# RWKV's main streams on TensorE in the order of the source, with the projections between them left free

## The chip, the cores and the metric

The kernel runs on one core of one Trainium2 chip. The metric is the device time of one execution in microseconds. The kernel before took 1292.87 us, the median of three runs (1289.9 to 1293.16 us). TensorE is called PE below, VectorE DVE, ScalarE ACT, GpSimd POOL and SyncE SP.

## The reference

One step of a one-layer hybrid encoder for 1024 prompt frames and 64 sample frames (with 512 cached ones). All branch columns come from one projection of the normalised input; three branches are gated and projected back:

```
u = rms_norm(h); z = u @ w_in                      # (1088, 1024) @ (1024, 5836)
A: RWKV-7 mixing, 8 heads of 64: a delta-rule state S (64 x 64 per head), frame by frame
     S = S * w_t + (S @ -kk_t) (kk_t * a_t)^T + v_t k_t^T ;  y_t = S @ r_t
B: forgetting attention (FoX), 8 heads, softmax(q k / 8 + c_t - c_s), s <= t
C: indexer scores, the top 256 keys of each frame, softmax attention over them with a T5 bias
h = h + concat(y_A * silu(g_A), y_B * silu(g_B), y_C * silu(g_C)) @ w_out ; y = rms_norm(h)
```

Outputs are y for prompt and sample, the new states and the new cache rows.

## The kernel before

**Stages.** After the input norm comes the indexer, then the RWKV stage with the top-k search beside it, then FoX, then the sparse attention and the output projection. The change concerns the RWKV stage.

**Projections.** `proj` (L154) multiplies 128 columns of w_in with 384 or 320 frames. For each of eight slices of 128 input features it issues three matmuls, a triple: bf16 weights with the low part of u, then the high and the low part of the weights with the high part of u. After a triple the generator yields. Projections wait in the deque `fill`; `pump(n)` adds n to a credit and issues one triple for each whole credit. In the RWKV stage's braids the credit grows by 0.7 per step, and by more in the last braids.

**RWKV in chunks.** The recurrence is computed in chunks of 64 frames, four chunks of one pair of heads to a unit: 16 units for the prompt and one for the sample. Each unit goes through five streams, written as generators: the preparation (`prep`: element-wise work on decay, rates and keys in `elem`, then the chunk's products in `chunk_rows`), `value_rows` (`rows`), the inversion of a triangular 64 x 64 matrix by doubling (`invert`, five levels), the sequential `chain` over the four chunks, and the `tail` with the group norm. In `invert`, PE products (L1500, L1507, transposes L1514) alternate with DVE updates of U, T and Y (L1538, L1543, L1547). In `chain` each chunk has three steps: L1588 and DVE's za (L1589); L1593 and DVE's copies of UV (L1598); and then

```
matmul(ch[.., c*64 ..], BA.., UV..)                        # L1601, both halves
scalar_tensor_tensor(self.state, ch[.., c*64 ..], ..)      # L1606, DVE
matmul(py = ch[.., 256 + c*64 ..], BA.., UV..)             # L1610, same PSUM bank as ch
matmul(py, QR.., S)                                        # L1612
```

Most fp32 matmuls stand twice in the profile, so that L1601 and L1610 have four entries for each chunk. The products of `elem`, `chunk_rows` and `value_rows` use one PSUM bank in turn (`ps_ga`), some of them `ps_tp`; the inversion has two (`ps_gb`).

**The braid.** `program` runs 19 braids. In braid u stand the tail of unit u-2, the chain of u-1, the inversion and the value rows of u, and the preparation of u+1. `braid` deals their steps by fractions: step k of a stream with n steps has the place (k + 0.5)/n, with n = 3 for the tail, 12 for the chain, 14 for the inversion, 10 for the preparation (it uses eight), and 2 for the value rows (place times 0.4). After each step come `note` and `pump`, and steps of the top-k search on DVE and ACT. The first preparation runs alone in a `weave`.

**What sets the order on an engine.** The program is not issued in the order of the source. The framework keeps a priority for each instruction (its place in the source) and orders each engine's queue by its own estimate of when operands and buffers are ready: the ready instruction of the highest priority first. Order edges constrain it: an edge says that one instruction stands behind another on its engine, without a wait. `tied` gives the instructions of a projection step a priority 1000 places later and ties the first PE instruction to the last one of the stream whose step came before (`behind`, which `note` keeps). So a projection does not stand ahead of that point, and may stand later. Between the main streams there is one set of edges: `in_order(at)` after L1442 keeps eight products of `chunk_rows` in their order.

Of the kernel before, what the change touches and what calls it, by code (L numbers as in the profile page):

```python
# [85 lines left out]
class K:  # L86
# [96 lines left out]
    def note(self, label):  # L183

        ins = self.nc.cur_bb.bb.instructions
        for i in ins[self.seen:] if label in TIES or not TIES else ():
            self.behind.setdefault(i.engine, {})[label if TIE else 0] = i.name
        self.seen = len(ins)

    def in_order(self, n):  # L190

        last = None
        for i in self.nc.cur_bb.bb.instructions[n:]:
            if i.engine == PE:
                if last is not None:
                    self.tc.add_manual_dep(i, last, mybir.DependencyInfo(
                        mybir.DependencyClass.NoSync, mybir.DependencyReason.DATA), reason="order of issue")
                last = i.name

    def pump(self, n):  # L200

        self.credit = min(self.credit + n, 8)
        while self.credit >= 1 and self.fill:
            self.mark(self.fill[0][0])
            if self.tied(self.fill[0][1], (PE,)):
                self.credit -= 1
            else:
                self.filled.add(self.fill.popleft()[0])
# [1201 lines left out]
    def chunk_rows(self, one, x):  # L1410

        nc = self.nc
        v, g, sc = nc.vector, nc.gpsimd, nc.scalar
        G = self.gring("ga", 1)
        QR, BK, ND = x["QR"], x["BK"], x["ND"]
        dg = self.dg

        BA = one.tile([P, 2, 4, 128], F32, tag="BA", name="BA", bufs=3)  # L1420
        BN = one.tile([P, 2, 4, 64], F32, tag="BN", name="BN", bufs=NBN)
        lo, hi = hv = (slice(0, 64), slice(64, 128))
        p1 = G()
        for c in range(4):
            self.turn(p1[:, c * P:c * P + P], BK[:, c, 0:2].rearrange("p a t -> p (a t)"))
        q1 = p1.rearrange("p (c h d) -> p c h d", h=2, d=64)
        sc.copy(BA[:, 0, :, 0:64], q1[:, :, 0])
        sc.copy(BA[hi, 1, :, 64:128], q1[lo, :, 1])
        sc.copy(BA[lo, 1, :, 64:128], q1[hi, :, 1])
        yield  # L1430
        am = self.con[:, C_AM:C_AM + P].rearrange("p (o x t) -> p o x t", o=1, x=2)
        ps = self.tp()
        nc.tensor.matmul(ps[:, :256], self.ones[:, C_BD - C_M:C_N - C_M], x["rk"], start=True, stop=True)
        x["vb"] = vb = one.tile([P, 4, 64], F32, tag="vb", name="vb", bufs=4)
        v.scalar_tensor_tensor(vb, ps[:, :256].rearrange("p (c t) -> p c t", t=64), 0.5, QR[:, :, 2], op0=OP.mult, op1=OP.mult)
        yield

        pm = G(), self.tp()
        at = len(nc.cur_bb.bb.instructions)
        for c in range(4):  # L1440
            for h in range(2):
                nc.tensor.matmul(pm[h][:, c * P:c * P + P], BK[hv[h], c, h:h + 2].rearrange("p a t -> p (a t)"),  # L1442
                                 QR[hv[h], c, 0:2].rearrange("p a t -> p (a t)"), start=True, stop=True)
        self.in_order(at)
        for h in range(2):
            q = pm[h].rearrange("p (c x t) -> p c x t", x=2, t=64)
            for i, dst in ((1, BN[:, h]), (0, BA[:, h, :, 64 - 64 * h:128 - 64 * h])):
                v.tensor_tensor(dst, q[:, :, i], am[:, :, i].broadcast_to([P, 4, 64]), op=OP.mult)
            g.tensor_scalar(dg(ND[:, 0], h), BN[hv[h], h], 1.0, 0.0, op0=OP.mult, op1=OP.add)
            g.tensor_tensor(dg(ND[:, 1], h), BN[hv[h], h], dg(ND[:, 0], h), op=OP.subtract)  # L1450
            if h == 0:
                yield
        x.update(BA=BA, BN=BN)
        yield
# [330 lines left out]
def program(ctx, tc, I, O):  # L1785
    s = K(ctx, tc, I, O)
    s.pproj = s.pool("pproj", bufs=2, space=PSUM)
    s.ptp = s.pool("ptp", bufs=1, space=PSUM)
    s.banks = itertools.cycle((s.proj_bank, s.proj_bank, s.tp))
    s.keep = s.pool("keep")  # L1790
    s.dram = s.pool("dram", space=DRAM)
    s.d_g = s.dram.tile([1024, NT], F32, tag="d_g", name="d_g")
    s.d_y = s.dram.tile([2, 4, P, NT], F32, tag="d_y", name="d_y")
    s.cp = s.pool("const")
    c1 = ExitStack()
    uw = s.pool("uw", ctx=c1)
    s.uH = uw.tile([P, KD, NT], F32R, name="uH")
    s.uL = uw.tile([P, KD, NT], BF16, name="uL")
    s.wraw = s.pool("wraw", bufs=NW, ctx=c1)
    s.wsp = s.pool("wsp", bufs=2, ctx=c1)  # L1800
    s.zp = s.pool("zp", bufs=2, ctx=c1)
    ci = ExitStack()
    s.ip = s.pool("idx", ctx=ci)
    s.ip2 = s.pool("idx2", bufs=2, ctx=ci)
    cx = ExitStack()
    s.load_x(cx)
    s.mark('norm')
    s.norm_in()
    s.mark('setup')
    s.setup()  # L1810
    cx.close()
    with ExitStack() as c2:
        s.lr = s.pool("lr", ctx=c2, right=True)
        s.zs = s.pool("zs", bufs=1, ctx=c2, right=True)
        s.scp = s.pool("scp", ctx=c2, right=True)
        s.tkp = s.pool("tkp", ctx=c2, right=True)
        s.junk = s.pool("junk", ctx=c2, right=True)
        s.free = True
        s.weave(("idx", s.indexer()), R_IDX[0], R_IDX[1])
        ci.close()  # L1820
        s.rwkv_pools(c2)
        s.need("a0")
        s.free = False
        for nm, w, j in (("a2", s.park_a, 2), ("a3", s.park_a, 3), ("b0", s.park_b, 0),
                         ("b1", s.park_b, 1), ("b2", s.park_b, 2), ("b3", s.park_b, 3)):
            s.fill.append((nm, w(j)))
        for j in range(4):
            s.fill.append((f"c{j}", s.park_c(j)))
        for j in range(4):
            s.fill.append((f"g{j}", s.park_cg(j)))  # L1830
        units = [[(hp, 4 * q + i) for i in range(4)] for hp in range(4) for q in range(4)] + [[(hp, 16) for hp in range(4)]]
        topk = s.topk()
        n = len(units)
        x = [dict(ND=s.ND[u % 2]) for u in range(n)]
        s.weave(("prep0", s.prepare(units[0], x[0])), 10, R_A)
        for u in range(n + 2):
            work = []
            if u >= 2:
                work.append(("tail", s.tail(s.one, x[u - 2]), 3, ()))
            if 1 <= u <= n:  # L1840
                work.append(("chain", s.chain(s.one, units[u - 1], x[u - 1]), NCH, ()))
            if u < n:
                work.append(("invert", s.chunk_invert(s.one, x[u]), 14, ()))
                work.append(("rows", s.value_rows(s.one, x[u], u == n - 1), 2, ()))
            if u + 1 < n:
                if u % 4 == 3 and u < 15:
                    s.need(f"a{u // 4 + 1}")
                work.append(("prep", s.prepare(units[u + 1], x[u + 1]), 10, ()))
            if u < n:
                work.append(("topk", topk, N_TOPK, (DVE, ACT)))  # L1850
            work = [w[:3] for w in work if w[0] != "topk"]
            if u:
                next(s.bias, None)
            s.free = u >= FE
            s.braid(work, R_T if u > n else R_END if len(work) < 3 and u else R_A / 10, ("topk", topk, N_TOPK, (DVE, ACT), work[-1][0] if SIDE < 0 else work[SIDE][0]) if u < n else None)
        for _ in topk:
            pass
        s.need("b0")
        for _ in range(PX):
            s.pump(8)  # L1860
        if FX:
            s.free = False
    s.lend = False
    s.shift_out()
    s.att_pools(ctx)
    def between():
        s.need("g3")
        c1.close()
        s.out_pools(ctx)
        w = s.load_wout(range(12))  # L1870
        s.mark("wout")
        for _ in range(WI):
            next(w)
        s.fill.append(("wout", w))

    operands = s.pool("operands", ctx=ctx, right=True)
    s.attention("att", itertools.chain(s.fox(operands), s.dsa(operands, between)),
                lambda: R_FOX if "c3" not in s.filled else RG if "g3" not in s.filled else R_DSA1)
    for i in (6, 7):
        s.fill.append((f"o{i}", s.output(i)))  # L1880
    s.need("o7")
# [64 lines left out]
```

## Time and profile before

| What | Value |
|---|---|
| Median of three runs | 1292.87 us |
| The profiled execution | 1289.49 us |
| Its span (first to last instruction) | 1286.6 us |
| Busy share PE, weight loads, DVE, ACT, POOL | 96, 73, 66, 61, 52% |
| Mean granted clock of TensorE | 0.991 |

The span is the time from the first to the last instruction of the profiled execution; 2.9 us of its time lie around it. Busy time is time in which an engine has an instruction in flight. Matmuls are pipelined, so that PE counts as busy where its matmuls overlap or where one is only finishing. "Idle before" is the time with nothing in flight before an instruction, put down to what ended it; "issue" is a wait for nothing that the profile shows.

### The profile page before, as it was taken

How to read it: one execution, taken by the hardware profiler on the slowest of the kernel's cores; microseconds unless marked ns; L12 is line 12 of the kernel's file. 1: busy time of each engine (PE TensorE's matmuls, PEld its weight loads, DVE VectorE, ACT ScalarE, POOL GpSimd, SP SyncE). 2: the span in 40 equal slices, each digit the busy share in tenths (PEclk: the TensorE clock that was granted, in tenths of full speed). 3: DMA queues.
4: the chain of work that ended last, by engine and by line, in shares of the span. 5: the costliest groups of instructions: out<-in, count | busy, mean ns of one | idle time of the engine just before them, and what ended most of it. 6: DMA issues, size and time to landing. Idle time of an engine off the chain costs nothing.

```text
span 1286.6 us, 29362 instructions
## 1 busy us (share of the span) xinstructions
PE 1230.5 (96%) x10563; PEld 941.8 (73%) x10563; DVE 843.0 (66%) x2487; ACT 780.3 (61%) x1762; POOL 671.7 (52%) x973
## 2 busy tenths in 40 slices
PE   7999999999999999988999989999999889999997
PEld 5777777777777777666777767888887756777764
DVE  7468458888887787998564136556665588666642
ACT  7345357788877888544344456676664587655531
POOL 6333444545545655646454555576666477444311
PEclk9999999999999999989999999999999999999999
DMA  8332421232332443325225389676756476534323
GB/s 231 108 104 68 138 85 52 68 100 71 90 96 73 125 132 105 116 83 170 90 73 162 115 233 268 191 217 201 200 155 183 130 217 171 146 104 114 87 82 95
DMA packets 171699, 168.77 MB, mean 131 GB/s; under 512 B 38641, under 2 KB 146209, under 8 KB 171426
## 3 DMA queue, kind: packets, MB, share of 16 engines
q1 hardware_dynamic: 171554, 166.91, 44.7%
q8 instruction: 83, 1.36, 0.4%
q14 instruction: 62, 0.51, 0.1%
HBM read 106.18 MB, written 62.25 MB: 131 GB/s over the span
## 4 chain that ended last, share of the span: by engine, by line
PE 78%; DVE 9%; DMA 6%; ACT 3%; issue 2%; SPq 1%; POOL 0%; DVEq 0%; POOLq 0%; ACTq 0%
PE pproj L154 37%; PE pproj L1726 7%; PE ps_pv L1005 5%; PE ps_atp L107 4%; PE ps_tp L1726 4%; PE ps_sc L974 2%; PE ps_sc L975 2%; PE ps_gb L1500 2%; PE ps_tp L107 1%; PE ps_gb L1507 1%; ACT junka L613 1%; PE ps_gc L1610 1%; PE ps_gc L1612 1%; PE ps_gc L1601 1%; PE ps_ga L107 1%
## 5 line engine op out<-in xcount | busy, mean ns | idle before, releaser
L154 PE MATMUL pproj<-uH,wh 128*128 128x384 f32 (+4 forms) x1088 | 491.4, 452 | 0.0
L154 PE MATMUL pproj<-uH,wl 128*128 128x384 f32 (+4 forms) x1088 | 361.6, 332 | 0.0
L154 PE MATMUL pproj<-uL,wb 128*128 128x384 bf16 (+4 forms) x1088 | 356.9, 328 | 0.8 <-DVE shift L818 0.5
L154 PEld LDWEIGHTS pproj<-uH,wh 128*128 128x128 f32 (+1 forms) x1088 | 215.8, 198 | 4.8 <-issue 0.7
L154 PEld LDWEIGHTS pproj<-uH,wl 128*128 128x128 f32 (+1 forms) x1088 | 206.5, 190 | 2.0
L154 PEld LDWEIGHTS <-wb 128*128 128x128 bf16 (+1 forms) x1088 | 105.8, 97 | 116.5 <-issue 80.5
L613 ACT ACTIVATE junka<-score,tk_tau 128x1024 f16<-128x1024 f32 (+4 forms) x160 | 149.5, 934 | 33.1 <-DVE junk L607 22.1
L926 POOL TENSOR_SCALAR S<-S,mx 128x128 f32<-128x128 f32 (+8 forms) x136 | 105.6, 780 | 84.1 <-DVE mx L925 62.6
L140 POOL TENSOR_TENSOR wl<-wraw,wh 128x256 fp32r<-128x256 f32 (+1 forms) x184 | 137.8, 780 | 5.8 <-ACT wh L137 4.8
L943 ACT CAST hl<-ps_atp 128x512 fp32r<-128x512 f32 (+3 forms) x184 | 93.6, 515 | 76.8 <-PE ps_atp L107 67.1
L944 DVE TENSOR_TENSOR hl<-ps_atp,hl 128x512 fp32r<-128x512 f32 (+3 forms) x184 | 109.7, 600 | 45.1 <-ACT hl L943 43.4
L921 ACT ACTIVATE S<-S,mx 128x128 f32<-128x128 f32 (+8 forms) x136 | 105.8, 778 | 39.6 <-DVE mx L917 36.1
L142 POOL TENSOR_SCALAR wb<-wraw 128x512 bf16<-128x512 f32 (+1 forms) x92 | 62.9, 701 | 114.3 <-PE pproj L154 66.9
L1005 PE MATMUL ps_pv<-hl,VS 128*128 128x256 f32 (+3 forms) x640 | 111.9, 286 | 7.6 <-ACT hl L943 3.4
L1005 PEld LDWEIGHTS ps_pv<-hl,VS 128*128 128x128 f32 (+1 forms) x640 | 88.7, 173 | 20.7 <-DVE hl L944 4.7
L107 PE MATMUL ps_atp<-ident,S 128*128 128x128 f32 x616 | 101.7, 276 | 1.1 <-DVE hl L944 0.6
L1171 POOL TENSOR_TENSOR cb<-nm,T 128x256 f32<-128x256 bf16 (+2 forms) x80 | 54.3, 685 | 54.5 <-DVE mx L917 52.7
L107 PEld LDWEIGHTS ps_atp<-ident,S 128*128 128x128 f32 x616 | 74.8, 141 | 7.8 <-issue 1.0
L137 ACT CAST wh<-wraw 128x1024 fp32r<-128x1024 f32 (+1 forms) x46 | 47.7, 1037 | 35.9 <-PE pproj L154 35.4
L1726 PE MATMUL pproj<-oh,gh 128*128 128x512 f32 x144 | 67.4, 490 | 0.8 <-ACT oh L1705 0.5
L1726 PE MATMUL pproj<-ol,gb 128*128 128x512 bf16 (+1 forms) x144 | 52.4, 386 | 0.9 <-DVE ol L1706 0.9
L1598 DVE COPY UV<-ps_gd 64x64 f32<-64x64 f32 x136 | 29.9, 220 | 28.7 <-PE ps_gd L1593 26.5
(387 smaller groups left out, 2845.2 us busy)
## 6 DMA issues: line engine op xcount, KB each, us to landing
wraw<-in_w_in_dram SPq DMA_DIRECT2D x45, 512.0 KB
oraw<-in_w_out_dram SPq DMA_DIRECT2D x12, 512.0 KB
out_dram<-rows SPq DMA_DIRECT2D x10, 512.0 KB
x<-in_x_prompt_dram SPq DMA_DIRECT2D x8, 512.0 KB
wt<-a_wa SPq DMA_DIRECT2D x16, 256.0 KB
b_v<-vs SPq DMA_DIRECT2D x8, 512.0 KB
VS<-b_v SPq DMA_DIRECT2D x8, 512.0 KB
d_y<-y SPq DMA_DIRECT2D x64, 64.0 KB
```

The costliest lines, as they stand in the source:

```text
L107: self.nc.tensor.transpose(out, x, self.ident[:n, :n])
L140: nc.gpsimd.tensor_tensor(l[:, k:k + 2, :n], raw[:, k:k + 2, :n], h[:, k:k + 2, :n], op=OP.subtract)
L142: nc.gpsimd.tensor_scalar(b[:, k:k + 4, :n], raw[:, k:k + 4, :n], 1.0, 0.0, op0=OP.mult, op1=OP.add)
L154: self.nc.tensor.matmul(ps[:n, :nt], a[:, k, :n], b[:, k, t0:t0 + nt], start=(k == 0 and i == 0), stop=(k == KD - 1 and i == 2))
L613: nc.scalar.activation(junk[:, :sc.shape[1]], sc, AF.Sign, bias=tf[:, j:j + 1], accum_out=cnt[:, j:j + 1])
L921: nc.scalar.activation(S[:, :kn], S[:, :kn], AF.Exp, bias=mx[:, nm - 1:nm], scale=-1.0, accum_out=mx[:, 6:7])
L926: nc.gpsimd.tensor_scalar(S[:, :kn], S[:, :kn], mx[:, 7:8], 0.5, op0=OP.mult, op1=OP.mult)
L943: nc.scalar.copy(ph[:kr, a:b], ps[:kr, a:b])
L944: nc.vector.tensor_tensor(pl[:kr, a:b], ps[:kr, a:b], ph[:kr, a:b], op=OP.subtract)
L1005: nc.tensor.matmul(pv[0:m, q0:256], VS[:, kb, 0:m], hl[:, x, o:o + w], start=kb == 0 and x == 0, stop=at[-1][0] == last and n == 3)
L1171: nc.gpsimd.tensor_tensor(o, x, y, op=OP.add)
L1726: nc.tensor.matmul(ps[hf][:n, :], parts[m // 4][q][:, m % 4, :n], self.wo[m][q // 2][:, hf * 512:hf * 512 + 512], start=m == 0 and q == 0, ...
```

## The change

`note` is called after each step of a main stream. With the change it ties, while `strict` is not None, every PE instruction that this step issued to the main streams' PE instruction before it, from the first preparation to the end of the last braid. Projection steps and the top-k search move `seen` past themselves, so that their instructions get no such edge. The edges after L1442 go into the general ones.

```diff
     def note(self, label):
         ins = self.nc.cur_bb.bb.instructions
+        if self.strict is not None:
+            self.strict = self.in_order(self.seen, self.strict or None)
         for i in ins[self.seen:] if label in TIES or not TIES else ():
...
-    def in_order(self, n):
-
-        last = None
+    strict = None
+
+    def in_order(self, n, last=None):
+
         for i in self.nc.cur_bb.bb.instructions[n:]:
             if i.engine == PE:
                 if last is not None:
                     self.tc.add_manual_dep(i, last, mybir.DependencyInfo(
                         mybir.DependencyClass.NoSync, mybir.DependencyReason.DATA), reason="order of issue")
                 last = i.name
+        return last
...
-        self.in_order(at)
+        if self.strict is None:
+            self.in_order(at)
...
         x = [dict(ND=s.ND[u % 2]) for u in range(n)]
+        s.strict = ""
         s.weave(("prep0", s.prepare(units[0], x[0])), 10, R_A)
...
             s.braid(work, ...)
+        s.strict = None
```

## Rows read from the trace of the kernel before

**Rows 1.** The page: busy time and share by engine, and the chain's engines.

```profile
PE 1230.5 (96%) x10563; PEld 941.8 (73%) x10563; DVE 843.0 (66%) x2487; ACT 780.3 (61%) x1762; POOL 671.7 (52%) x973
...
PE 78%; DVE 9%; DMA 6%; ACT 3%; issue 2%; SPq 1%; POOL 0%; DVEq 0%; POOLq 0%; ACTq 0%
```

**Rows 2.** Stretches: length, busy us of PE, loads, DVE, ACT, POOL, clock, DMA, GB/s.

```profile
148.00:735.00 587.00, 565.62 (x6515) 424.63 (x6514) 422.94 (x1311) 379.76 (x881) 316.50 (x480) 0.99 0.33 101
500.00:600.00 100.00, 89.08 (x1000) 66.80 (x1000) 89.27 (x249) 51.48 (x124) 58.06 (x80) 0.97 0.36 111
535.00:550.00 15.00, 11.67 (x134) 8.64 (x133) 13.75 (x31) 7.37 (x16) 12.29 (x14) 1.00 0.31 96
550.00:565.00 15.00, 12.90 (x129) 9.71 (x129) 12.84 (x30) 4.60 (x11) 5.62 (x11) 0.77 0.36 118
```

**Rows 3.** PE's groups by line, 148:735 us: busy us, mean ns | idle before, releasers.

```profile
L154 PE MATMUL pproj<-uH,wh 128*128 128x384 f32 (+1 forms) x609 | 275.7, 453 | 0.0
...
L1507 PE MATMUL ps_gb<-T,ND 128*128 128x64 f16 x476 | 33.1, 195 | 2.4 <-DVE T L1543 1.6 <-ACT T L1552 0.8
L1500 PE MATMUL ps_gb<-U,Y 64*64 64x64 f16 x816 | 30.5, 194 | 2.2 <-DVE Y L1538 1.0 <-DVE Y L1556 0.9
L1601 PE MATMUL ps_gc<-UV,BA 128*64 128x64 f32 x272 | 25.7, 247 | 1.6 <-DVE UV L1598 1.5
L1610 PE MATMUL ps_gc<-UV,BA 128*64 128x64 f32 x272 | 22.8, 246 | 3.0 <-DVE S L1606 2.3 <-DVE s_end L1606 0.5
...
L1500 PE MATMUL ps_gb<-Y,U 64*64 64x64 f16 x544 | 21.1, 197 | 1.1 <-DVE Y L1538 0.9
...
L1514 PE MATMUL ps_gb<-identh,U 64*64 64x64 f16 x272 | 10.2, 195 | 1.6 <-DVE U L1547 1.1
```

**Rows 4.** PE's timeline, 304.3:309 us: start us, us, engine, line, count, idle before.

```profile
306.42 0.34 PE L1601 MATMUL ps_gc<-UV,BA 128*64 128x64 f32 x4
306.68 0.31 PE L1500 MATMUL ps_gb<-Y,U 64*64 64x64 f16 x8
306.83 0.29 PE L1500 MATMUL ps_gb<-U,Y 64*64 64x64 f16 x8
307.06 0.34 PE L154 MATMUL pproj<-uL,wb 128*128 128x384 bf16 x1
...
307.40 0.34 PE L154 MATMUL pproj<-uH,wl 128*128 128x384 f32 x1
307.58 0.34 PE L154 MATMUL pproj<-uL,wb 128*128 128x384 bf16 x1
...
307.93 0.34 PE L154 MATMUL pproj<-uH,wl 128*128 128x384 f32 x1
308.20 0.34 PE L1610 MATMUL ps_gc<-UV,BA 128*64 128x64 f32 x4
308.46 0.27 PE L1612 MATMUL ps_gc<-S,QR 64*64 64x64 f32 x2
```

**Rows 5.** DVE's timeline in the same stretch.

```profile
307.08 0.28 DVE L1606 SCALAR_TENSOR_TENSOR S<-ps_gc,Pt,sp 128x64 f32<-128x64 f32 x1
```

**Rows 6.** PE's timeline, 429:440 us.

```profile
430.95 0.28 PE L1316 MATMUL ps_ga<-wt,wabh 128*128 128x256 f32 x1
...
433.94 0.34 PE L1601 MATMUL ps_gc<-UV,BA 128*64 128x64 f32 x4
434.69 0.34 PE L1610 MATMUL ps_gc<-UV,BA 128*64 128x64 f32 x4 [0.41 <-DVE S L1606]
...
437.86 0.29 PE L1514 MATMUL ps_gb<-identh,U 64*64 64x64 f16 x8
```

**Rows 7.** PE's groups by line, 500:600 us.

```profile
L1316 PE MATMUL ps_ga<-wt,wabh 128*128 128x256 f32 x6 | 2.0, 341 | 2.8 <-issue 2.8
L1486 PE MATMUL ps_ga<-UV,BN 64*64 64x64 f32 x48 | 2.0, 224 | 1.9 <-DVE QR L1390 1.9
...
L107 PE MATMUL ps_ga<-ident,BK 128*128 128x128 f32 x12 | 1.9, 277 | 2.2 <-DVE BK L1393 2.2
```

## The prediction

> **What bounds the kernel now.** The page's busy shares come first. PE has matmuls in flight for 96% of the span, and the chain of work that ended last runs through PE for 78% of it [rows 1]. The projections (L154) are the largest part of that, and the change leaves their number and their work alone. So the question is how much of PE's time in the RWKV stage is waiting, and whether another order of the same matmuls waits less.
>
> Next is the table by stretches [rows 2]. The stage reaches from 148 us to 735 us, and PE is busy for 565.62 of its 587 us: it idles 21.4 us. Of these, 10.9 us lie between 500 and 600 us, where DVE is as full as PE (89.27 against 89.08 us). Outside it, 10.5 us of idle time are spread over 487 us. By these rows there is no large hole to close; anything above some 2% would have to come from waits that the busy column does not show.
>
> Then the groups by line in that stage [rows 3] say in front of which matmuls PE idles: the inversion (L1507 2.4 us, L1500 2.2 and 1.1, L1514 1.6) and the chain (L1601 1.6, L1610 3.0), each time released by DVE, or once by ACT. That is 8.9 us without L1610.
>
> Last, two stretches of PE's timeline show which order the scheduler made. In [rows 6] the low-rank product L1316 of the next unit's preparation starts at 430.95 us, seven us before the transposes L1514 at 437.86 us that open the inversion. In the source the preparation's first step of a braid comes after the inversion's first step. So the streams do float against each other now, and the order that the change prescribes is a different one: the preparation, the value rows and the tail go back by some us, and the inversion comes forward.
>
> **The change, part by part.** It adds no instruction, no transfer and no byte. Each PE instruction of the main streams gets an order edge to the one before it in the source. SP's and POOL's queues get no edge, and nor do DVE's and ACT's; their orders follow only as the scheduler's times move. What changes is what can stand in front of a matmul that has to wait. So far that was any ready stream or a projection; from now on it is a projection alone, and all later main matmuls queue behind the waiting one, with the DVE and ACT work that they feed.
>
> (a) *Chain and inversion waits.* In the braid, the 14 steps of an inversion, the 12 of a chain, the preparation, the tail and the value rows are dealt by their fractions, so that two steps of one stream have two or three others between them. The 68 chunks of the chain (272 matmuls of L1601 in fours, [rows 3]) take 587/68 = 8.6 us each at most, or about 2.9 us per chain step; an inversion step has 587/17/14 = 2.5 us. What a step needs is shorter: from L1601 at 306.42 to the end of DVE's state update it is 0.94 us [rows 4, 5]. With the source's spacing most of these waits should go. I count two thirds of the visible 8.9 us: -6 us. As much again I take for waits hidden under matmuls in flight: a group that follows a projection starts 0.27 us after its last matmul (307.93 to 308.20), a following projection 0.18 us after it (307.40 to 307.58) [rows 4], so 0.09 us per entry is not visible as idle. 609 triples in runs of two are some 305 entries, 27 us; of these I call 6 us waits, an estimate. Part (a): -12 us, between 0 and -18 (all of 8.9, twice).
>
> The Trainium skill, page "Perfetto Trace Analysis", section "Identifying the Most-Contended Engine", warns that the matmul busy share is no good measure of how near TensorE is to its limit, since pipelined instructions overlap. By the busy rows alone the gain ends at 21.4 us; by that rule it need not. The 0.09 us of [rows 4] agrees with the rule in kind; no run here sizes it yet.
>
> (b) *The wait that the order itself makes.* In `chain`, L1601 and L1610 stand in one step with nothing between them, and L1610 writes the PSUM bank from which DVE is reading for the state (L1606). Now other streams stand between: at 306.42 L1601, then two groups of L1500 and two projection triples, then L1610 at 308.20 [rows 4]. Where nothing fitted in, L1601 came at 433.94 and L1610 at 434.69, after 0.41 us of idle time that DVE's state update ended [rows 6]. Tied to the source, only projections can fill that hole. Its size without the group's own 0.26 us (308.20 to 308.46 [rows 4]) is 0.75 - 0.26 = 0.49 us where DVE comes at once, and 0.94 + 0.05 - 0.26 = 0.73 us where it is as late as in [rows 5], the 0.05 being the least that I allow from DVE's end to PE's start; on average 0.61 us. Sixty-eight such holes are 41 us if none is filled, and nothing if all are, which would also remove the 3.0 us that L1610 waits today. One triple takes 0.52 us (307.06 to 307.58 [rows 4]) and so covers the small hole, and two cover the large one. Supply: 609 triples over 68 chunks, nine per hole. The projections stay free to be late, so the scheduler can put them there. They stand behind every ready main matmul in priority, so they should collect until a main matmul is not ready, and this is the surest place. I take 12 holes of 68 as unfilled, those whose triples went into an earlier hole: 12 x 0.61 - 3.0 = +4 us. Bounds: -3 and +38.
>
> (c) *More changes between projections and main groups.* Dealt as in the source, at most one triple follows a step; [rows 4] has two together. A run more costs the 0.09 us above. Up to 305 more runs would be 27 us; as holes still collect triples, I take 20 more: +2 us, between 0 and +27.
>
> (d) *The preparation, later by seven us.* What hides it is the time until the next inversion: the preparation's last matmuls come at 0.65 of a braid (the seventh of its ten slots), and the next inversion starts 0.39 braids later; at 34.5 us per braid (587/17) that is 13 us. Cost nothing; if the cover were gone, the inversion would start late by what is missing, and the braid behind it. The tail and value rows feed nothing sooner than the next braid: nothing. The attention and output stages after 735 us keep their code: nothing, within their scatter.
>
> The sum: -12 + 4 + 2 = -6 us. The profiled execution took 1289.49 us (span 1286.6 us and 2.9 us around it), 3.4 us below the median of 1292.87. So 1283.5 us for that execution, and 1287 us against the median.
>
> **Rivals.** *The holes at L1610 stay open* (slower). The same waits decide, with the other sign: a strict queue makes PE wait in more places in the scheduler's eyes too, the triples go to the first of these, and L1610 finds none left. With half of the holes open it is 34 x 0.61 - 3 = +18 us, with (a) down to -8 and (c) at +4: +14 us, 1307 us. It decides from 21 open holes on, where 21 x 0.61 - 3 eats the 10 us that (a) and (c) leave. For it: nothing else may stand between the two lines any more. Against it: nine triples per hole.
>
> *The stretch that DVE fills gets worse* (slower). Between 500 and 600 us PE idles 10.9 us, of which 6.9 before three lines of the preparation and the value rows (L1316 2.8, L107 2.2, L1486 1.9 [rows 7]). Where DVE is late, the change makes every stream wait for the latest one. In this stretch PE's clock fell too: after 535 to 550 us with 11.67 us busy of 15, the granted clock of the next 15 us was 0.77 [rows 2], so part of it ran at the lower of the two levels, which cost 0.23 x 15 = 3.5 us. Twice the idle time and twice that loss: 10.9 + 3.5 = +14 us, with (a) at -6: 1301 us. The Trainium skill, page "TensorE: Matmul & The Clock Gate", section "HAM oscillation — how this bites in real kernels", has such a loss come back at every pause that is long enough; the trace agrees for this one stretch; over the whole stage the mean clock is 0.99 of the upper level [rows 2].
>
> *Work bounds PE, and the waits only move* (no change). PE is busy for 565.6 of 587 us; what the chain no longer waits for, the ring of one PSUM bank behind L1316, L107 and L1486 or the hole of (b) takes back. Time 1293 us.
>
> *The change does not act.* The order would have to be the source's already; [rows 6] show that it is not. Chance nearly nil; counted with no change.
>
> **How the numbers follow.** Faster as summed: 0.42, with a range of its own of 1272 to 1289 us ((a) at -18, (b) at -3 and (c) at 0 give -21). No change: 0.23. Holes at L1610: 0.23. DVE's stretch: 0.12. A measurement of this kernel can tell about 0.3% (3.9 us) from no change, so faster is 0.42, the same 0.23 and slower 0.35. The range for 8 in 10 is 1271 to 1311 us: the best sum below, and above the first rival with some 40 holes open.
>
> **What would show it.** In the changed kernel the idle time before L1601, L1500, L1507 and L1514 falls from 8.9 us to about 3, L1610's grows to about 7, PE's timeline has L1316 of the next unit behind the opening L1514, and between L1601 and L1610 stand triples of L154 and nothing else. Step (b) is wrong if L1610's idle time goes beyond 12 us; step (a) is wrong if the other lines keep theirs. The prediction as a whole is wrong if the stage 148 to 735 us gets longer, or if its gain is given back after 735 us.

## The result: 3.9% slower, and where the time went

The changed kernel takes 1341.41 us (median of six runs, 1337.74 to 1347.03) against 1291.41 us (1288.54 to 1293.91) beside it: a ratio of 1.0393, interval 1.0364 to 1.0422. The forecast was 1287 us, at most 1311, and faster. The sign was wrong, and the time is outside the range.

The code of the changed stage stands four or five lines lower: L1601 is now L1606, L1610 is L1615, L1612 is L1617, the state update L1606 is L1611, L1500 is L1505, L1507 is L1512, L1514 is L1519, L1316 is L1320.

The page after, answering [rows 1]: busy time by engine, and the engines of the chain that ended last.

```profile
PE 1244.8 (93%) x10563; PEld 949.3 (71%) x10563; DVE 838.7 (63%) x2487; ACT 779.0 (58%) x1762; POOL 660.7 (49%) x973
...
PE 69%; DVE 11%; ACT 8%; DMA 5%; issue 4%; POOL 2%; SPq 0%; DVEq 0%; POOLq 0%; ACTq 0%
```

The instructions are the same. PE gave up nine points of the chain, mostly to ACT (3 to 8%), DVE (9 to 11%) and issue (2 to 4%): PE now waits for others more often.

To see where, both stages need one end. I take the transpose of the frame shift that closes the stage; it starts at 755.7 us before and at 807.9 us after. Stretches of the kernel before (length, busy us of PE, weight loads, DVE, ACT, POOL, clock, DMA, GB/s):

```profile
148.00:755.70 607.70, 585.31 (x6633) 439.19 (x6633) 425.26 (x1322) 389.31 (x906) 330.93 (x505) 0.99 0.35 106
755.70:1286.60 530.90, 506.37 (x3141) 399.18 (x3138) 322.13 (x946) 312.41 (x702) 277.96 (x385) 0.99 0.57 161
```

The same of the changed kernel, then three stretches inside its stage:

```profile
148.00:807.90 659.90, 598.55 (x6651) 444.11 (x6650) 421.98 (x1326) 390.34 (x906) 323.23 (x506) 0.97 0.32 97
...
807.90:1340.20 532.30, 507.11 (x3131) 401.58 (x3128) 321.61 (x943) 310.24 (x702) 273.75 (x385) 0.98 0.57 162
...
500.00:600.00 100.00, 82.08 (x998) 60.41 (x995) 85.54 (x245) 54.38 (x128) 52.03 (x77) 0.98 0.36 117
...
640.00:660.00 20.00, 19.86 (x253) 14.87 (x248) 13.28 (x38) 9.46 (x24) 10.93 (x17) 1.00 0.36 116
660.00:680.00 20.00, 16.58 (x147) 11.85 (x145) 5.97 (x20) 7.12 (x17) 10.56 (x17) 0.74 0.35 111
```

The rest of the kernel takes 530.9 and 532.3 us: nothing is lost there. The stage is 52.2 us longer. PE's idle time in it rises from 607.7 - 585.3 = 22.4 to 659.9 - 598.6 = 61.3 us (+38.9), its busy time by 13.3 us. DVE and ACT do the same work (425 to 422, 389 to 390 us). The busy time grew mostly because of the clock: TensorE ran 41.0 us of the stage at 1.2 GHz instead of 2.4, before 6.8 us, by the trace's clock records. Its price is an estimate: each matmul that starts in such a stretch is set against the mean, at 2.4 GHz, of the same line followed by the same next line, from one start to the next with no idle time between. By this the low stretches took 15.8 us longer than the same work at 2.4 GHz, before 3.1 us. So 52.2 = 38.9 of waiting + 12.7 of clock + 0.6 of the rest.

PE's groups by line in that stage, answering [rows 3] (busy us, mean ns, idle us before with releasers):

```profile
L1512 PE MATMUL ps_gb<-T,ND 128*128 128x64 f16 x476 | 33.2, 196 | 2.3 <-DVE T L1548 2.2
L1505 PE MATMUL ps_gb<-U,Y 64*64 64x64 f16 x816 | 30.9, 197 | 1.2 <-DVE Y L1561 0.8 <-DVE Y L1543 0.4
L1606 PE MATMUL ps_gc<-UV,BA 128*64 128x64 f32 x272 | 23.8, 249 | 0.0
L1615 PE MATMUL ps_gc<-UV,BA 128*64 128x64 f32 x272 | 23.5, 253 | 35.0 <-DVE S L1611 30.1 <-DVE tk_need L672 2.6 <-DVE s_end L1611 1.8
...
L1505 PE MATMUL ps_gb<-Y,U 64*64 64x64 f16 x544 | 21.6, 200 | 0.0
...
L1320 PE MATMUL ps_ga<-wt,wabh 128*128 128x256 f32 (+1 forms) x39 | 13.5, 354 | 6.2 <-ACT UV L1484 6.1
...
L1519 PE MATMUL ps_gb<-identh,U 64*64 64x64 f16 x272 | 10.6, 199 | 1.6 <-DVE U L1552 1.6
```

One line has 35.0 of the 61.3 us: L1615, the y products that wait for DVE's state update. It had 3.0 us. Two of its places, in PE's timeline (start us, us, engine, line, count, idle before), answering [rows 4, 6]:

```profile
312.40 0.34 PE L154 MATMUL pproj<-uH,wl 128*128 128x384 f32 x1
312.67 0.34 PE L1606 MATMUL ps_gc<-UV,BA 128*64 128x64 f32 x4
313.41 0.34 PE L1615 MATMUL ps_gc<-UV,BA 128*64 128x64 f32 x4 [0.41 <-DVE S L1611]
...
320.09 0.47 PE L154 MATMUL pproj<-uH,wh 128*128 128x384 f32 x1
320.50 0.34 PE L1606 MATMUL ps_gc<-UV,BA 128*64 128x64 f32 x4
320.76 0.45 PE L154 MATMUL pproj<-uH,wl 128*128 128x384 f32 x1
322.27 0.34 PE L1615 MATMUL ps_gc<-UV,BA 128*64 128x64 f32 x4 [1.07 <-DVE S L1611]
```

And DVE in front of the second, answering [rows 5]:

```profile
320.23 0.80 DVE L611 TENSOR_SCALAR_CACHE_REDUCE junk<-scores,tk_tau 64x576 f16<-64x576 f32 x1
...
320.95 0.41 DVE L1453 TENSOR_TENSOR BN<-ps_tp,con 128x256 f32<-128x256 f32 x1
321.29 0.41 DVE L1453 TENSOR_TENSOR BA<-ps_tp,con 128x256 f32<-128x256 f32 x1
321.62 0.41 DVE L1543 TENSOR_TENSOR Y<-ps_gb,con 128x256 f16<-128x256 f32 x1
321.95 0.27 DVE L1611 SCALAR_TENSOR_TENSOR S<-ps_gc,Pt,sp 128x64 f32<-128x64 f32 x1
```

At 312.67 the hole is bare: DVE comes at once, the next L1615 starts 0.74 us behind L1606, and no triple stands between; the last matmul of one, at 312.40, stands ahead of L1606. At 320.50 the state update stands on DVE behind a pass of the top-k search, two masking products (L1453) and a Y update, and starts 1.45 us after L1606; the last matmul of one triple covers a part, and PE waits 1.07 us. Over the 68 holes, counted in the trace (line numbers of before):

| Between L1601 and L1610, 68 chunks | before | after |
|---|---|---|
| Mean time from the first to the second | 1.96 us | 1.30 us |
| L1601 to the end of the state update | 1.13 us | 1.20 us |
| End of the state update to L1610 | 0.83 us | 0.11 us |
| Matmuls in between other than L154, all holes | 960 | 18 |
| Triples per hole; holes without one | 1.46; 15 | 0.63; 34 |

Before, 14 matmuls of other streams covered each hole, and the y products came when PE got to them. Of the 960, 20 are transposes of projected rows, which belong to the projections and get no tie; the 18 after are such transposes too. Now only projections may stand there, and half of the holes have no triple. The built queue of the changed kernel tells where the triples are: for 27 of the 34 empty holes one was dealt right before the chain's step, and it stands ahead of L1606, whose own wait it fills (L1601 had 1.6 us of idle time, L1606 has 0.0).

### The profile page after: what moved, and what is told of

It is laid out like the page before. It is cut to its first block, busy times and chain, and to the rows that moved or that the text cites. A ratio compares the mean times of both kernels' runs of the same rounds, so it can differ in the third digit from the quotient of the medians.

```text
span 1340.2 us, 29337 instructions
## 1 busy us (share of the span) xinstructions
PE 1244.8 (93%) x10563; PEld 949.3 (71%) x10563; DVE 838.7 (63%) x2487; ACT 779.0 (58%) x1762; POOL 660.7 (49%) x973
## 4 chain that ended last, share of the span: by engine, by line
PE 69%; DVE 11%; ACT 8%; DMA 5%; issue 4%; POOL 2%; SPq 0%; DVEq 0%; POOLq 0%; ACTq 0%
PE pproj L154 30%; PE pproj L1731 7%; PE ps_pv L1009 5%; PE ps_atp L107 5%; PE ps_tp L1731 4%; ACT junka L617 3%; PE ps_sc L978 3%; PE ps_sc L979 2%; DVE junk L611 1%; PE ps_gc L1615 1%; PE ps_gb L1505 1%; PE ps_tp L107 1%; DMA cQ<-c_q0l 1%; PE ps_gb L1512 1%; PE ps_gc L1617 1%
## 5 line engine op out<-in xcount | busy, mean ns | idle before, releaser
L154 PE MATMUL pproj<-uH,wh 128*128 128x384 f32 (+4 forms) x1088 | 498.7, 458 | 0.0
L154 PE MATMUL pproj<-uH,wl 128*128 128x384 f32 (+4 forms) x1088 | 364.1, 335 | 0.0
L154 PE MATMUL pproj<-uL,wb 128*128 128x384 bf16 (+4 forms) x1088 | 360.7, 332 | 2.1 <-DVE zg L799 0.9
L154 PEld LDWEIGHTS pproj<-uH,wh 128*128 128x128 f32 (+1 forms) x1088 | 218.9, 201 | 7.2 <-issue 2.2
L154 PEld LDWEIGHTS pproj<-uH,wl 128*128 128x128 f32 (+1 forms) x1088 | 209.4, 192 | 2.0
L154 PEld LDWEIGHTS <-wb 128*128 128x128 bf16 (+1 forms) x1088 | 107.5, 99 | 118.0 <-issue 80.2
L617 ACT ACTIVATE junka<-score,tk_tau 128x1024 f16<-128x1024 f32 (+4 forms) x160 | 149.3, 933 | 37.4 <-DVE junk L611 23.2
L1175 POOL TENSOR_TENSOR cb<-nm,T 128x256 f32<-128x256 bf16 (+2 forms) x80 | 51.3, 648 | 58.4 <-DVE mx L921 54.8
L1454 POOL TENSOR_SCALAR ND<-BN 64x256 f16<-64x256 f32 x34 | 13.6, 400 | 104.9 <-DVE BN L1453 103.7
L1615 PE MATMUL ps_gc<-UV,BA 128*64 128x64 f32 x272 | 23.5, 253 | 35.0 <-DVE S L1611 30.1
```

Of the source, the lines that this page charges most:

```text
L154: self.nc.tensor.matmul(ps[:n, :nt], a[:, k, :n], b[:, k, t0:t0 + nt], start=(k == 0 and i == 0), stop=(k == KD - 1 and i == 2))
L617: nc.scalar.activation(junk[:, :sc.shape[1]], sc, AF.Sign, bias=tf[:, j:j + 1], accum_out=cnt[:, j:j + 1])
L1175: nc.gpsimd.tensor_tensor(o, x, y, op=OP.add)
```

## The experiments

"Stage" is the time to the same transpose, less that of the kernel before (755.7 us) or after (807.9 us), in one profiled execution. That execution can lie off its kernel's median (strict_pair's 6.9 us above, strict_y_loose's 4.9 us below), so a few us between two stages decide nothing.

**Is it the hole?** The first pair of edits takes the hole out of the strict order in two ways. One moves the y products, which read the old state, ahead of L1606:

```diff
+            py = ...; 2 x matmul(py, BA.., UV..); 2 x matmul(py, QR.., S)
             matmul(ch[.., c*64 ..], BA.., UV..)
             scalar_tensor_tensor(self.state, ...)
-            py = ...; 2 x matmul(py, BA.., UV..); 2 x matmul(py, QR.., S)
```

> The changed kernel, with the y products of a chunk (L1610 and L1612 of before) moved ahead of the state product L1601, so that nothing on PE waits for the DVE read of that bank inside the step. Theory A (the wait that the order makes between L1601 and L1610 is the loss): the idle time before the y product falls from 35 us to under 5 us, and the time to 1285 to 1305 us. Theory B (any strict order of all streams loses, since each late DVE or ACT result holds up every stream, and the y product is only where it shows): at least 1325 us, with 25 us or more of the idle time reappearing before other lines.

The other leaves them in place and gives them no edge:

```diff
-            if i.engine == PE:
+            if i.engine == PE and i.name not in self.loose:     # the eight y matmuls
```

> The changed kernel, with the code in its old order but the four y products of a chunk left out of the order edges, so that other streams can again stand between L1601 and L1610. Theory A: 1285 to 1310 us, at least 30 us faster than the changed kernel. Theory B: 1325 us or more, since all other streams stay in lockstep.

Measured: 1329.03 us, ratio 1.0279 (1.0254 to 1.0305), stage 13.9 us shorter than after; and 1324.50 us, 1.0245 (1.0228 to 1.0262), 22.5 us shorter. The second one's row by stretch:

```profile
148.00:785.40 637.40, 596.38 (x6635) 443.40 (x6634) 424.24 (x1322) 389.37 (x906) 328.83 (x505) 0.98 0.33 100
```

And its groups of PE (five to seven lines further down than before; L1617 are the y products):

```profile
L1513 PE MATMUL ps_gb<-T,ND 128*128 128x64 f16 x476 | 32.9, 195 | 4.9 <-DVE T L1549 4.7
L1506 PE MATMUL ps_gb<-U,Y 64*64 64x64 f16 x816 | 30.8, 196 | 9.2 <-DVE Y L1544 3.9 <-DVE Y L1562 3.5 <-DVE tk_need L673 1.5
L1617 PE MATMUL ps_gc<-UV,BA 128*64 128x64 f32 x272 | 22.9, 247 | 2.4 <-DVE S L1612 1.9 <-DVE s_end L1612 0.2
L1321 PE MATMUL ps_ga<-wt,wabh 128*128 128x256 f32 (+1 forms) x39 | 13.4, 351 | 4.5 <-ACT UV L1485 4.4
```

The wait at the y products is gone (35.0 to 2.4 us), and still PE idles 637.4 - 596.4 = 41.0 us. The inversion's waits come up: L1506 has 9.2 us, 1.2 after, L1513 4.9. Theory A fails in both runs. Theory B's time is met by the first and missed by half a microsecond by the second; of the 25 us that it wanted to see reappear before other lines, some 13 did. By the stages the hole costs 22.5 of 52.2 us; by the medians, each beside its kernel before, 50.0 - 32.0 = 18.0 us. Some 30 us come from elsewhere in the strict order, which the hole had partly hidden: a stream that waits at L1615 gives the next ones time.

**The hole alone, in the free order.** The kernel before, with the chain's third step as one block on PE: it stands behind the last matmul that each stream issued before it, and all main matmuls issued later stand behind it.

```diff
+            for last in self.behind.get(PE, {}).values():
+                self.behind_of(made[0], last)     # made: PE's part of the step
+            self.in_order(b0)
+            self.next_bar = made[-1].name         # later PE instructions stand behind it
```

> The kernel before, with one part of the change alone: the third step of each chunk of the chain (L1601, L1610, L1612) is one block on PE, behind the last matmul of every other stream dealt before it and ahead of every one dealt after it; between these blocks all streams float as before. Theory A: slower than before by at least 25 us (1316 us or more), with 25 us or more of idle time before L1610. Theory B: under 1305 us, since the streams can still pass each other between the blocks.

Measured: 1353.75 us, 1.0490 (1.0439 to 1.0541), stage 62.8 us longer than before.

```profile
L1518 PE MATMUL ps_gb<-T,ND 128*128 128x64 f16 x476 | 32.9, 195 | 21.0 <-ACT T L1563 11.4 <-DVE T L1554 9.4
...
L1622 PE MATMUL ps_gc<-UV,BA 128*64 128x64 f32 x272 | 23.4, 251 | 28.3 <-DVE S L1618 25.2 <-DVE s_end L1618 1.4 <-DVE tk_ge L682 1.2
```

Sixty-eight barriers are enough to lose more than the whole change. The y products wait nearly as in the changed kernel (L1622, 28.3 us; L1615 had 35.0), and a second wait appears at L1518 in the inversion, which can no longer pass them. Theory A's numbers are met, but this is a barrier for all streams and not the hole alone, so it shows that such a block costs this much, and not how the 52 us divide.

**The moved y products in the free order.**

> The kernel before with the y products moved ahead of L1601, without any new order edge. Both theories: within 6 us of before (1285 to 1297 us): it takes away the 3.0 us of idle time before L1610 and makes the new state about 0.5 us later in each of 68 chunks, which the other streams cover.

Measured: 1307.04 us, 1.0108 (1.0092 to 1.0124): 17.1 us of stage, a miss. PE idles 20.0 us, 2.4 less than before; its busy time rose by 19.5 us, with 3.4 us more at the low clock. The rows show where. Before, the second pair of y products (L1612) runs side by side with the next chunk's first products (L1588). In the kernel before, beside the 308.46 of [rows 4]:

```profile
308.48 0.27 PE L1588 MATMUL ps_gd<-S,QR 64*64 64x64 f32 x2
308.57 0.23 PE L1612 MATMUL ps_gc<-S,QR 64*64 64x64 f32 x2
308.58 0.22 PE L1588 MATMUL ps_gd<-S,QR 64*64 64x64 f32 x2
```

With the y products moved (now L1602 and L1604, with the state product at L1607):

```profile
307.25 0.33 PE L1588 MATMUL ps_gd<-S,QR 64*64 64x64 f32 x4
...
311.05 0.33 PE L1604 MATMUL ps_gc<-S,QR 64*64 64x64 f32 x4
311.31 0.34 PE L1607 MATMUL ps_gc<-UV,BA 128*64 128x64 f32 x4
```

Before, 230 of the 272 entries of L1612 start within 0.06 us of one of L1588; moved, none does. From each start to PE's next one, idle time left out, the two lines together take 34.9 us instead of 21.2. So moving the y products has a price of its own, 13.7 us of the 17.1, and the 13.9 us that it gains in the strict order understate the hole: against this control the strict order costs 1329.03 - 1307.04 = 22.0 us.

**Which streams' edges cost the rest?** Only the chain's and the inversion's, with loose y products and the edges after L1442 put back; then only the other three streams':

```diff
-        if self.strict is not None:
+        if self.strict is not None and label in ('chain', 'invert'):                      # first
+        if self.strict is not None and label in ('prep0', 'prep', 'rows', 'tail'):        # second
```

> Only the inversion and the chain are tied to each other in the order of the source (the y products L1610 and L1612 of before left free, as in strict_y_loose, so that their wait is out of the comparison); preparation, value rows and tail float as in the kernel before. Theory C (the rest of the loss, 1324.5 against 1292.5 us in strict_y_loose, comes from the two serial streams waiting for each other): 1315 us or more. Theory D (it comes from tying preparation, value rows and tail, which share the one-bank rings ps_ga and ps_tp): under 1303 us.

> The complement: only preparation, value rows and tail are tied to each other in the order of the source; inversion and chain float. Theory C: under 1303 us. Theory D: 1315 us or more, with the added idle time before the matmuls into ps_ga and ps_tp.

Measured: 1311.82 us, 1.0139 (1.0102 to 1.0176), stage +23.5 us over before; and 1302.61 us, 1.0069 (1.0043 to 1.0096), +12.1 us. Theory C's bound for the first run is missed by 3 us, that for the second is met; theory D fails. Neither group carries the whole loss: the chain and the inversion have about two parts of three. Whether the parts add up is open: the stages make 35.6 us against the 29.7 of all five with loose y, the medians 16.4 + 7.2 = 23.6 against 32.0. In the first, PE idles before the inversion (L1512 8.3 us, L1505 6.2 and 3.1) and the y products (5.5); in the second before other lines (a transpose of the tail's Yt 6.6, the y products 5.0, the chain's L1593, which was L1588 before, 3.5). The waits sit at whichever matmul is late, and everything behind it on PE waits too.

**Are there too few triples?** The rate at which projections are dealt into the braids, 0.7 per step, is set to 1.0 in the strict and in the free kernel:

```diff
-            ... R_END if len(work) < 3 and u else R_A / 10, ...
+            ... R_END if len(work) < 3 and u else 1.0, ...
```

> The changed kernel with 1.0 instead of 0.7 projection triples dealt per step of a braid. Theory E (the strict order leaves PE without anything to run: projections go to PE as soon as they are dealt, so that none is left for the holes): idle time in the stage falls from 61 us by at least 20 us, and the whole time from 1341 to under 1325 us, since the triples are taken from the stage behind. Theory F (the waits lie on the streams' own path, and triples between them make it longer): the stage grows by what the triples take and the time stays at 1335 us or more.

> The kernel before with 1.0 instead of 0.7 triples per step, the control for strict_rate10: PE idles 22 us only in the stage, so both theories expect little, 1283 to 1300 us.

Measured: 1365.57 us, 1.0547 (1.0517 to 1.0576) and 1352.20 us, 1.0442 (1.0413 to 1.0471). The whole time says little: the attention stage misses the projections that now come early, and both lose there (at 1.0 its clock is 0.92). The free kernel's time was a miss, since I had left that out. The stage tells what was asked. Its row in the strict kernel:

```profile
148.00:853.90 705.90, 676.60 (x7211) 503.41 (x7210) 425.96 (x1319) 419.25 (x960) 376.86 (x573) 0.99 0.35 110
```

And in the free one:

```profile
148.00:849.40 701.40, 688.24 (x7218) 509.70 (x7218) 433.43 (x1319) 416.08 (x961) 381.54 (x574) 0.99 0.36 111
```

With 2487 projection matmuls instead of 1933 in the stage the strict order costs 705.9 - 701.4 = 4.5 us of it, not 52.2. PE's idle time there falls from 61.3 to 29.3 us, as theory E expected; the whole time, which was to be under 1325 us, did not follow. The holes now have 1.50 triples each, 15 have none, and L1615's idle time is 15.0 us. In the whole time the strict order still costs 1365.57 - 1352.20 = 13.4 us. So more triples cover most of what it costs in the stage.

The other way, 0.5 per step, one run each:

> The changed kernel with 0.5 triples per step. Only the length of the RWKV stage counts, against free_rate05. With 1.0 the strict order made the stage 4.5 us longer (853.9 against 849.4 us at its end), with 0.7 52 us (807.9 against 755.7). Theory E (the strict order costs what the triples cannot fill): the difference at 0.5 is at least 55 us, with more than 80 us of PE idle time. Theory F (a fixed cost of the strict order's own path, which 1.0 hid by chance): 35 to 50 us, not more than at 0.7.

> The kernel before with 0.5 triples per step, the control. The stage gets shorter by up to 60 us if PE's work bounds it (Theory E), less if the streams' own waits do; PE idle time in the stage 22 to 45 us.

Measured: 1397.33 and 1354.49 us. The stages end at 778.2 and 732.8 us: 45.4 us apart. PE idles 89.8 us in the strict stage, 53.4 in the free one (more than the 45 expected), with 78.5 and 51.2 us at the low clock. The difference did not grow beyond 52 us; the free kernel too runs short of triples (31 of its holes have none, 15 at 0.7). That the cost rises steadily as the triples get fewer is refuted; it is small where they abound and stays near 50 us below.

**Room for other streams in the hole.** A `yield` between the state update and the y products, with the dealing adapted (16 steps, 0.635 triples per step), in both orders:

```diff
             scalar_tensor_tensor(self.state, ...)
+            yield
             py = ...
-NCH=12
+NCH=16
```

> The changed kernel with the third step of a chunk cut in two by a yield, so that in the source, too, steps of other streams and a dealt triple stand between L1601 and L1610 (the rate is lowered from 0.7 to 0.635 per step, so that the same number of triples is dealt). Theory A' (this wait is a third of the loss, as strict_y_loose says, and the rest is the lockstep of the other streams): idle time before L1610 from 35 us to under 10 us, time 1315 to 1330 us. Theory B (the wait only moves to the next line): 1335 us or more.

> The kernel before with the same cut and rate: the streams float anyway, so both theories expect 1283 to 1303 us.

Measured: 1336.11 us, 1.0327 (1.0308 to 1.0346), and 1309.34 us, 1.0135 (1.0107 to 1.0163). Groups of the strict one:

```profile
L1512 PE MATMUL ps_gb<-T,ND 128*128 128x64 f16 x476 | 33.2, 196 | 9.8 <-DVE T L1548 8.8 <-ACT T L1557 1.0
...
L1616 PE MATMUL ps_gc<-UV,BA 128*64 128x64 f32 x272 | 23.2, 250 | 4.4 <-DVE S L1611 4.2
...
L1320 PE MATMUL ps_ga<-wt,wabh 128*128 128x256 f32 (+1 forms) x39 | 13.9, 365 | 10.0 <-ACT UV L1484 9.9
```

The hole is filled (L1616, 4.4 us), the stage 14.0 us shorter than after. Still the whole time misses the bound of theory A' and meets that of theory B: the waits appear at L1512 and L1320. The free kernel is a miss too, 6 us above its range, so the `yield` and the new dealing cost 16 us by themselves; against this control the strict order costs 1336.11 - 1309.34 = 26.8 us. In this order, covering one wait exposed the next one.

**Are the three other streams dealt too late?** Their places 0.15 of a braid earlier, with loose y products:

```diff
-        order = sorted(((k + 0.5) / n * (0.4 if ...), j) ...
+        order = sorted(((k + 0.5) / n * (0.4 if ...) - (0.15 if work[j][0] in ("tail", "rows", "prep") else 0), j) ...
```

> strict_y_loose with preparation, value rows and tail dealt 0.15 braids earlier in the source, about as far as they ran ahead of the inversion in the kernel before. Theory G (the particular order of the source loses, not the strictness): 1312 us or less, against 1324.5 for strict_y_loose. Theory H (strictness itself loses, whatever the order): 1320 us or more.

Measured: 1358.33 us, 1.0520 (1.0502 to 1.0539); the stage is 38.5 us longer than with their usual places.

```profile
L1513 PE MATMUL ps_gb<-T,ND 128*128 128x64 f16 x476 | 32.9, 195 | 15.4 <-DVE T L1549 12.1 <-ACT T L1558 2.5 <-ACT T L1540 0.4
...
L1321 PE MATMUL ps_ga<-wt,wabh 128*128 128x256 f32 (+1 forms) x39 | 13.8, 361 | 14.5 <-ACT UV L1485 14.5
```

Earlier by this much is worse: L1321 waits 14.5 us for ACT's UV, and the inversion 15.4. It meets theory H's bound but does not show H, since it is one other order and not the one of before: its preparation starts 5.1 to 10.2 us ahead of the inversion's opening transposes (median 5.9), that of the kernel before 3.2 to 16.6 us (median 12.0).

**Is it the search on DVE and ACT?** The search is not dealt into the braids but issued after them, in both orders, one run each:

```diff
-            s.braid(work, rate, ("topk", topk, ...) if u < n else None)
+            s.braid(work, rate, None)
```

> The changed kernel with the top-k search issued after the last braid instead of beside the braids, which takes its work off DVE and ACT in the stage; only the end of the RWKV stage counts, against free_topk_last. Theory Q (late answers from loaded DVE and ACT queues are what the strict order cannot bear): the strict stage is at most 26 us longer than the free one, against 52 us with the search. Theory L (the bare latencies of the steps): at least 40 us longer.

> The kernel before with the same move, the control. Its stage should end at 735 to 760 us, since PE's work bounds it but for the stretch from 500 to 600 us, which loses its DVE load.

Measured: 1333.87 and 1301.69 us, stages at 799.9 and 767.3 us: 32.6 us apart, between the two expectations; the free stage ends 7 us after its range. The edit missed its aim: the search holds no matmul, so the scheduler still set it into the stage, and earlier (its last selection ran at 554 and 557 us instead of 609 and 602), and DVE is busy for 416 and 424 us there, much as before. That the strict order lost 8 us less and the free one 11.6 more leaves the question open.

## Why the prediction was wrong

**Step (b) failed.** It took 12 of 68 holes as unfilled and +4 us, because of nine triples per hole, which "should collect until a main matmul is not ready". They do not collect. In the queues of both kernels, as built, a projection stood a median of about seven main matmuls behind its dealt place before, and two after: it follows almost where it is dealt, and the supply per hole is what falls between the two lines, not nine. In the trace 34 holes have no triple and L1615 idles 35.0 us. The hole's size was nearly right: the 34 without a triple have 23.4 us of idle time, 0.69 each against 0.61; the others, which I counted as closed, have 11.6 more. The upper bound, +38 us, holds the measured +32.0. The whole stage in the prediction's terms: +32.0 at the y products, -3.8 at the lines of (a), +10.7 before other lines (L1320 alone 3.4), +12.7 of clock and +0.6 of the rest make the 52.2 us; the prediction had -6.

The first rival had the mechanism: the triples go to the wait ahead of L1606, and L1615 finds none left. That half of the holes, its example, is 34 to the hole is luck. Its 1307 us came out too low by two things that it did not have, besides those 11.6 us. One is the other streams. With the y products loose the strict order still costs 29.7 us of the stage; tying the chain and the inversion costs 23.5, the other streams 12.1. The prediction put this at nothing: I had read a strict queue as spacing that *removes* waits; a queue in the source's order also passes one stream's lateness to all the others behind. The other is the clock: 12.7 us. PE idled in many short pieces, and in thin stretches its clock was lower: 16.58 us busy of 20 at 660 us, with a granted clock of 0.74 there, against 1.00 in the 20 us ahead with 19.86 us busy. The second rival priced this effect at 3.5 us. The Trainium skill, page "TensorE: Matmul & The Clock Gate", section "A second HAM failure mode: psum-queue depth-cycling", describes, in another kernel, micro-idles of TensorE between matmul groups that are frequent enough to make its clock go up and down; the trace agrees, here with 41.0 against 6.8 us at the lower level.

**Step (a) was right in kind.** The idle time before L1601, L1500, L1507 and L1514 was to fall from 8.9 to about 3 us; it is 0.0 + 1.2 + 2.3 + 0.0 + 1.6 = 5.1 us. In the runs that cover the hole it comes back (L1506 9.2 us with loose y products): it was low because PE waited at L1615 instead. So (a)'s gain was partly a loan. Of the hidden 6 us no trace here gives a figure apart from (c): what idle time and clock leave is +0.6 us for both.

**Step (c) did not occur.** Projection runs in the stage number 278 before and 273 after; the prediction had twenty more.

**Step (d) held in its order and its cover, not in its price.** The next unit's L1320 now stands behind the transposes L1519 that open the inversion:

```profile
426.69 0.29 PE L1519 MATMUL ps_gb<-identh,U 64*64 64x64 f16 x8
...
427.05 0.39 PE L1320 MATMUL ps_ga<-wt,wabh 128*128 128x256 f32 x1
```

[rows 6] showed a small case: over the units the preparation ran 3.2 to 16.6 us ahead before, with a median of 12.0 instead of seven; now it starts 0.2 to 3.9 us behind. The cover held all the same: no opening group waits, and the preparation's last products (L1446) end 5.5 to 13.1 us ahead of it. But the preparation, the value rows and the tail were to cost nothing, and tying these three alone cost 7.2 us by the medians (12.1 us of stage). After the stage nothing changed (530.9 and 532.3 us).

**The stretch that DVE fills** got worse, as the second rival said, by 17.9 - 10.9 = 7.0 us of idle time between 500 and 600 us, by the changed kernel's row above; but 10.6 us of it stand before L1615, and the lines of [rows 7] lost theirs (L1320 has 1.4).

A rule that bears on this hole was at hand: the Trainium skill, page "Perfetto Trace Analysis", section "Matmuls", wants independent matmul groups in different PSUM banks, so that emptying one bank overlaps the next group. L1606 and L1615 share a bank; the trace agrees, with 0.74 us between them where nothing else stood (312.67 to 313.41). The free order had covered this with 940 matmuls of other streams; no run put the two lines into different banks.

**Shown and open.** Shown by runs: of the 50.0 us between the medians the wait at the y products costs 18 to 28 (18.0 by the loose edges; 50.0 - 26.8 = 23.2 and 50.0 - 22.0 = 28.0 by the two kernels that remove it, each against its free control), the rest of the order 22 to 32; with more triples the strict order costs 4.5 us of the stage. The clock's 12.7 us are worked out from the records, not from a run that holds the clock. Not shown: that strictness as such loses. PE's queue is fixed when the program is built, in the free kernel too: in both, the 5440 matmuls of L154 and of the inversion's three lines stand in the trace exactly as in the built queue. So what lost is the source's order against the one that the scheduler picks, and no run tied the scheduler's own. Open: how much of DVE's and ACT's lateness is their queues' load and how much bare latency. The state update starts 34.5 us later in sum than if it always came 0.41 us after L1606 (before: 29.8), which says that the load is there in both kernels; the run meant to remove it did not. No version ran faster than the kernel before.

## What to carry to other kernels

Before an engine's order is tied, list the places where two neighbours of the source wait for each other through another engine, and price each as open: a filler covers a hole only if the queue puts it into that hole, not because there are many of them in the stage. Here the order that the scheduler picked hid both the latency and the lateness of the other engines; the source's passed them on to every stream behind, and waits that looked gone were often only moved. A surplus of free work covered more of the stage than moving the tied steps did, but it was borrowed: the stages behind missed it, and the whole time rose from 1341 to 1366 us.

## What the runs showed of the hardware

Many short waits came with a cost beyond their sum: 92 idle pieces of TensorE, the longest 2.56 us and 61.3 us in all (before: 61, 1.56 and 22.4 us), went with 34.2 us more at 1.2 GHz, by the estimate above about 13 us on top. The idle sum alone does not set it: with the earlier places PE idled 65.5 us of the stage in 111 pieces and ran 30.7 us of it at 1.2 GHz.

The 64 x 64 matmuls of L1612 and L1588 run side by side where they stand next to each other: they start 0.02 us apart (308.46 and 308.48) and take 0.27 us each. Moving one of them away made the free kernel's stage 17.1 us longer with *less* idle time (20.0 against 22.4 us): the lost overlap, 13.7 us, shows as busy time.
